# Attention over 64 heads on one core: Exp over three PSUM banks at a time, shared rotating banks, split opening and split last tile

## The chip, the core and the metric

The kernel runs on one core of a Trainium2 chip. The metric is the device time of one execution in microseconds (us); lower is better. A core has five engines that run at the same time and wait for each other through semaphores: TensorE (PE, matrix multiplication; PEld is its weight load), VectorE (DVE), ScalarE (ACT), GpSimd (POOL) and SyncE (SP, which here issues DMAs). Matrix products land in PSUM, a memory of 128 partitions with eight banks of 512 fp32 values each.

## The reference

Softmax attention for 8 batches of 8 heads, 512 queries and 512 keys of 64 values each, in fp32:

```python
def reference(q, k, v):               # each [8, 8, 512, 64]
    scale = 1.0 / np.sqrt(q.shape[-1])
    scores = np.einsum('bhqd,bhkd->bhqk', q, k) * scale
    scores = scores - scores.max(axis=-1, keepdims=True)
    attn = np.exp(scores)
    attn = attn / attn.sum(axis=-1, keepdims=True)
    return np.einsum('bhqk,bhkd->bhqd', attn, v).astype(np.float32)
```

## The kernel before

The 64 heads are worked as 32 pairs. For a pair `g`, one DMA each brings q, k and v of both heads (256 KB each, `load`, L56), five pairs ahead at the start of every pair. POOL casts them to fp16 (`cast`: q and k at L69, v at L73). The v tile has a 65th column of ones, so that the product with it also gives the row sums of the softmax. PE transposes q and k in eight 128x128 pieces into one PSUM bank (`transpose`, L87), and DVE copies the result to the tile `tqk` (L90), where head A lies on partitions 0 to 63 and head B on 64 to 127.

The work then goes by steps `t`: a step is one chunk of 128 keys (`c`, four of them) of one pair. `scores` (L102) makes two matmuls, one for each head, into the two banks of a tile `st`, with keys on the partitions and the 512 queries along the row. `softmax` (L112) is one ACT instruction: exp of both banks, 1024 values per partition, written as fp16 to `pt`. `weigh` (L123) multiplies, for each head and each quarter of the queries, the chunk of `pt` with v: eight matmuls of 65 columns that add into two banks `ps_o`, one for each head, over the four chunks. After the fourth chunk `finish` has DVE take the reciprocal of the sums (L141) and multiply (L142), and SP store the pair (L148).

PSUM is used as follows: `ps_t` one bank, `ps_st` two tiles of two banks, `ps_o` three banks; all eight are taken. No maximum is subtracted; exp is taken of the scaled scores.

The order on each engine is that of the code (`manual_schedule`): in every step exp of `t`, scores of `t + 1`, weigh of `t - 1`, and in the first three chunks of a pair two or three transposes of pair `g + 2`. So PE has a little of each kind of work in each step. An engine takes its instructions strictly in that order, and the tile pools place the waits: `scores(t + 1)` waits until exp of `t - 1` has emptied its two banks.

Of the kernel before, what the change touches and what calls it, by code (L numbers as in the profile page):

```python
# [1 line left out]

# [5 lines left out]

FP32 = mybir.dt.float32
FP16 = mybir.dt.float16  # L10

EXP = mybir.ActivationFunctionType.Exp
AluOp = mybir.AluOpType


@with_exitstack
def kernel(
    ctx: ExitStack,
    tc: tile.TileContext,
    q: bass.AP,  # L20
    k: bass.AP,
    v: bass.AP,
    out: bass.AP,
):
# [10 lines left out]
    NV = 4  # L35

    cpool = ctx.enter_context(tc.tile_pool(name="att_const", bufs=1))
    lpool = ctx.enter_context(tc.tile_pool(name="att_load", bufs=6))
    xpool = ctx.enter_context(tc.tile_pool(name="att_x", bufs=3))
    ppool = ctx.enter_context(tc.tile_pool(name="att_p", bufs=6))  # L40
    opool = ctx.enter_context(tc.tile_pool(name="att_out", bufs=3))
    pspool = ctx.enter_context(tc.tile_pool(name="att_psum", bufs=1, space=bass.MemoryType.PSUM))

    def src(x, g):
        b, h = g // ppb, 2 * (g % ppb)
        return x[b, h : h + 2].rearrange("h (p i) d -> p h (i d)", i=NI)

    raw = {}

    def load(g):  # L50
        if g >= n_pairs:
            return
        t = []
        for nm, x in (("q", q), ("k", k), ("v", v)):
            r = lpool.tile([P, 2, NI * D], FP32, tag=f"{nm}32", name=f"{nm}32_{g}")
            nc.sync.dma_start(out=r, in_=src(x, g))  # L56
            t.append(r)
        raw[g] = t

    vps = [cpool.tile([P, 2, NI, W], FP16, name=f"vp{n}") for n in range(NV)]  # L60
    halves = {}

    def cast(g):
        if g >= n_pairs:
            return
        q32, k32, v32 = raw.pop(g)
        qk = xpool.tile([P, 2, NI, P], FP16, tag="qk", name=f"qk_{g}")
        for n, r in enumerate((q32, k32)):
            nc.gpsimd.tensor_copy(  # L69
                out=qk[:, n].rearrange("p i (h d) -> p i h d", d=D),  # L70
                in_=r.rearrange("p h (i d) -> p i h d", d=D),
            )
        nc.gpsimd.tensor_copy(  # L73
            out=vps[g % NV][:, :, :, 0:D],
            in_=v32.rearrange("p h (i d) -> p h i d", d=D),
        )
        halves[g] = qk

    tps, tqk = {}, {}

    def transpose(g, lo, hi):
        if g >= n_pairs:
            return
        if lo == 0:
            tps[g] = pspool.tile([P, 2, NI, P], FP16, tag="ps_t", bufs=1, name=f"tps_{g}")
        for n in range(lo, hi):
            nc.tensor.transpose(tps[g][:, n // NI, n % NI, :], halves[g][:, n // NI, n % NI, :], ident)  # L87
        if hi == 2 * NI:
            tqk[g] = xpool.tile([P, 2, S], FP16, tag="tqk", name=f"tqk_{g}")
            nc.vector.tensor_copy(out=tqk[g], in_=tps[g])  # L90

    st, pt, ops = {}, {}, {}
    n_steps = n_pairs * NI

    def scores(t):
        if t >= n_steps:
            return
        g, c = divmod(t, NI)
        st[t] = pspool.tile([P, 2, S], FP32, tag="ps_st", bufs=2, name=f"st_{t}")
        for h in range(2):  # L100
            po = D * h
            nc.tensor.matmul(  # L102
                st[t][:, h, :],
                tqk[g][po : po + D, 1, c * P : (c + 1) * P],
                tqk[g][po : po + D, 0, :],
                start=True,
                stop=True,
            )

    def softmax(t):  # L110
        pt[t] = ppool.tile([P, 2, S], FP16, tag="pt", name=f"pt_{t}")
        nc.scalar.activation(out=pt[t], in_=st.pop(t), func=EXP, scale=scale)  # L112

    def weigh(t):
        g, c = divmod(t, NI)
        if c == 0:
            ops[g] = [
                pspool.tile([P, NI, W], FP32, tag="ps_o", bufs=3, name=f"o_{g}_{h}")
                for h in range(2)
            ]  # L120
        for h in range(2):
            for i in range(NI):
                nc.tensor.matmul(  # L123
                    ops[g][h][:, i, :],
                    pt[t][:, h, i * P : (i + 1) * P],
                    vps[g % NV][:, h, c, :],
                    start=(c == 0 and i == 0),
                    stop=(c == NI - 1),
                    skip_group_check=True,
                )  # L130
        del pt[t]
        if c == NI - 1:
            finish(g)

    def finish(g):
        b, hA = g // ppb, 2 * (g % ppb)
        o_sb = opool.tile([P, 2, NI, D], FP32, tag="o_sb", name=f"osb_{g}")
        rcp = opool.tile([P, 2, NI], FP32, tag="rcp", name=f"rcp_{g}")
        for h in range(2):
            o = ops[g][h]  # L140
            nc.vector.reciprocal(out=rcp[:, h, :], in_=o[:, :, D : D + 1])  # L141
            nc.vector.tensor_tensor(  # L142
                out=o_sb[:, h],
                in0=o[:, :, 0:D],
                in1=rcp[:, h, :].broadcast_to([P, NI, D]),
                op=AluOp.mult,
            )
        nc.sync.dma_start(  # L148
            out=out[b, hA : hA + 2].rearrange("h (p i) d -> p h (i d)", i=NI),
            in_=o_sb,  # L150
        )
        del ops[g]

    AHEAD = 5
    with tc.manual_schedule():
        load(0)
        load(1)
        ident = cpool.tile([P, P], FP16, name="ident")
        make_identity(nc, ident)
        for n in range(NV):  # L160
            nc.vector.memset(vps[n][:, :, :, D:W], 1.0)  # L161
        warm = cpool.tile([P, 1], FP32, name="warm")
        nc.vector.memset(warm, 0.0)
        nc.scalar.activation(out=warm, in_=warm, func=EXP, scale=scale)  # L164
        for g in range(2, AHEAD):
            load(g)
        cast(0)
        cast(1)
        transpose(0, 0, 2 * NI)
        scores(0)  # L170
        transpose(1, 0, 2 * NI)
        for t in range(n_steps):
            g, c = divmod(t, NI)
            if c == 0:
                cast(g + 2)
                load(g + AHEAD)
            softmax(t)
            scores(t + 1)
            if t > 0:
                weigh(t - 1)  # L180
            if c < NI - 1:
                transpose(g + 2, 3 * c, min(3 * c + 3, 2 * NI))
        weigh(n_steps - 1)


# [1 line left out]
_INS = ['q', 'k', 'v']  # L187
_OUTS = [((8, 8, 512, 64), 'float32')]


# [23 lines left out]
```

## Time and profile before

| | |
|---|---|
| median of 3 runs | 133.63 us (133.58 to 134.33) |
| the profiled execution, its own time | 133.69 us |
| span of its instructions | 131.8 us |
| ACT busy | 119.4 us, 91% of the span, 130 instructions |
| PE busy | 112.5 us, 85%, 1536 matmuls |
| DVE busy | 58.1 us, 44% |
| POOL busy | 56.9 us, 43% |
| DMA | 33.82 MB, 257 GB/s on average |

The busy time of an engine is the union of its instructions. An ACT instruction that is handed over while the one ahead still runs counts from its hand-over, so the mean of one exp is longer than the distance from one to the next; the distance is what counts in a row of them. The chain of waits follows the work that ended last back to the start: a line of it says from when on, and how long, which instruction held the end back. Times in views are from the start of the span.

### The profile page before, as it was taken

The page shows a single profiled execution, that of the slowest core. Times are in us where ns is not written, and L with a number is a line of the kernel's source. Part 1 is how long each engine was busy: PE and PEld are TensorE (multiplying, and loading weights), DVE is VectorE, ACT ScalarE, POOL GpSimd, SP SyncE. Part 2 cuts the span into 40 slices and gives each one's busy share as a digit, 9 for nine tenths or more (in the row PEclk, how much of TensorE's full clock was granted, in tenths as well). Part 3 has the DMA queues.
Part 4 walks back from the last instruction along what each step waited for, and adds up shares of the span by engine and source line. Part 5 has one row for each costly group of instructions (what it writes and reads, how often), then busy time and mean ns, then how long its engine had stood idle before and what let it go on. Part 6 is the DMA issues. An engine that isn't in the chain of part 4 may idle for free.

```text
span 131.8 us, 3961 instructions
## 1 busy us (share of the span) xinstructions
PE 112.5 (85%) x1536; PEld 71.2 (54%) x1536; DVE 58.1 (44%) x165; ACT 119.4 (91%) x130; POOL 56.9 (43%) x102
## 2 busy tenths in 40 slices
PE   0479999999999999999999999999999999998840
PEld 0225665656556556565655656556565665655530
DVE  0220545544455445554445544554444554455230
ACT  4056999999999999999999999999999999999960
POOL 2578874444455554444445555444444555100000
PEclk9999999999999999999999999999999999999995
DMA  4999999989889879969988989969999982122222
GB/s 116 298 343 349 348 353 371 360 263 296 288 290 308 280 239 306 318 174 341 355 274 291 310 247 286 310 210 274 359 293 307 292 267 86 55 80 80 85 82 80
DMA packets 34836, 33.82 MB, mean 257 GB/s; under 512 B 2049, under 2 KB 34817, under 8 KB 34817
## 3 DMA queue, kind: packets, MB, share of 16 engines
q1 hardware_dynamic: 34816, 33.56, 79.3%
q8 instruction: 12, 0.20, 0.7%
q14 instruction: 8, 0.06, 0.1%
HBM read 25.17 MB, written 8.39 MB: 255 GB/s over the span
## 4 chain that ended last, share of the span: by engine, by line
ACT 72%; issue 10%; PE 8%; DMA 4%; SPq 2%; DVE 1%; POOL 0%
ACT pt L112 72%; DMA q<-in_q_dram 4%; PE st L102 4%; PE o L123 3%; SPq L56 2%; PE tps L87 1%; DVE osb L142 1%; POOL qk L69 0%; DVE rcp L141 0%
## 5 line engine op out<-in xcount | busy, mean ns | idle before, releaser
L112 ACT ACTIVATE pt<-st 128x1024 f16<-128x1024 f32 x128 | 117.9, 1197 | 7.1 <-PE st L102 7.0
L102 PE MATMUL st<-tqk 64*128 64x512 f16 x256 | 51.1, 387 | 9.0 <-ACT pt L112 6.0
L123 PE MATMUL o<-vp,pt 128*128 128x65 f16 x1024 | 54.2, 196 | 0.8 <-ACT pt L112 0.7
L123 PEld LDWEIGHTS <-pt 128*128 128x128 f16 x1024 | 38.5, 98 | 30.1 <-issue 29.0
L73 POOL CAST vp<-v 128x512 f16<-128x512 f32 x32 | 19.8, 619 | 52.8 <-PE o L123 51.1
L90 DVE COPY tqk<-tps 128x1024 f16<-128x1024 f16 x32 | 22.1, 692 | 36.0 <-PE tps L87 36.0
L87 PE MATMUL tps<-ident,qk 128*128 128x128 f16 x256 | 31.0, 227 | 5.4 <-POOL qk L69 5.2
L102 PEld LDWEIGHTS <-tqk 64*128 64x128 f16 x256 | 22.2, 93 | 19.4 <-issue 6.1
L142 DVE TENSOR_TENSOR osb<-o,rcp 128x256 f32<-128x256 f32 x64 | 27.1, 424 | 2.5 <-DMA out_dram<-osb 0.3
L141 DVE RECIPROCAL rcp<-o 128x4 f32<-128x4 f32 x64 | 11.3, 177 | 31.4 <-PE o L123 31.4
L69 POOL CAST qk<-q 128x512 f16<-128x512 f32 x32 | 19.7, 616 | 3.2 <-DMA q<-in_q_dram 3.0
L87 PEld LDWEIGHTS <-qk 128*128 128x128 f16 x256 | 16.5, 101 | 7.0 <-POOL qk L69 7.0
L69 POOL CAST qk<-k 128x512 f16<-128x512 f32 x32 | 19.7, 617 | 0.5
L164 ACT ACT_TABLE_LOAD x1 | 1.3, 1283 | 0.7 <-PEq L198 0.7
L161 DVE MEMSET vp<- 128x8 f16 x4 | 0.2, 65 | 0.8 <-PEq L198 0.8
masks.py:197 POOL MEMSET ident<- 128x128 f16 x1 | 0.2, 205 | 0.3 <-POOLq L198 0.3
masks.py:199 POOL TENSOR_SCALAR_AFFINE_SELECT ident<-ident 128x128 f16<-128x128 f16 x1 | 0.3, 294 | 0.1
L164 ACT ACTIVATE warm<-warm 128x1 f32<-128x1 f32 x1 | 0.2, 202 | 0.0
L198 POOL MEMSET const-float32-0.0<- 128x1 f32 x1 | 0.1, 100 | 0.2 <-issue 0.2
L198 POOL MEMSET const-bfloat16-1.0<- 128x1 bf16 x1 | 0.1, 103 | 0.0
L198 POOL MEMSET const-uint8-127<- 128x1 uint8 x1 | 0.1, 102 | 0.0
L198 POOL MEMSET const-float32-1.0<- 128x1 f32 x1 | 0.1, 100 | 0.0
(1 smaller groups left out, 0.1 us busy)
## 6 DMA issues: line engine op xcount, KB each, us to landing
q<-in_q_dram SPq DMA_DIRECT2D x32, 256.0 KB, 4.1
k<-in_k_dram SPq DMA_DIRECT2D x32, 256.0 KB, 4.4
v<-in_v_dram SPq DMA_DIRECT2D x32, 256.0 KB, 4.7
out_dram<-osb SPq DMA_DIRECT2D x32, 256.0 KB, 3.3
```

What stands on the lines that cost most here:

```text
L56: nc.sync.dma_start(out=r, in_=src(x, g))
L69: nc.gpsimd.tensor_copy(out=qk[:, n].rearrange("p i (h d) -> p i h d", d=D), in_=r.rearrange("p h (i d) -> p i h d", d=D),)
L73: nc.gpsimd.tensor_copy(out=vps[g % NV][:, :, :, 0:D], in_=v32.rearrange("p h (i d) -> p h i d", d=D),)
L87: nc.tensor.transpose(tps[g][:, n // NI, n % NI, :], halves[g][:, n // NI, n % NI, :], ident)
L90: nc.vector.tensor_copy(out=tqk[g], in_=tps[g])
L102: nc.tensor.matmul(st[t][:, h, :], tqk[g][po : po + D, 1, c * P : (c + 1) * P], tqk[g][po : po + D, 0, :], start=True, stop=True,)
L112: nc.scalar.activation(out=pt[t], in_=st.pop(t), func=EXP, scale=scale)
L123: nc.tensor.matmul(ops[g][h][:, i, :], pt[t][:, h, i * P : (i + 1) * P], vps[g % NV][:, h, c, :], start=(c == 0 and i == 0), stop=(c == NI ...
L141: nc.vector.reciprocal(out=rcp[:, h, :], in_=o[:, :, D : D + 1])
L142: nc.vector.tensor_tensor(out=o_sb[:, h], in0=o[:, :, 0:D], in1=rcp[:, h, :].broadcast_to([P, NI, D]), op=AluOp.mult,)
L164: nc.scalar.activation(out=warm, in_=warm, func=EXP, scale=scale)
L198: nc = _bacc.Bacc("TRN2", target_bir_lowering=False, num_devices=1)
```

## The change

The unit of the softmax is now one head's chunk (512 values, one bank), 256 of them, in the same sequence as before (head A and head B of chunk 0, of chunk 1, and so on). They are taken in groups: one of two units, 84 of three, two of one. `scores`, `softmax` and `pt` go by groups, so a group can hold units of two pairs, and a group's heads are A, B, A or B, A, B. `ps_st` is two tiles of three banks. The two banks that are left, `ps_x`, rotate between all other users: the eight transposes of a pair take one, the output of one head takes the next.

The transposes of a pair are therefore issued in one run of eight, and `attend` issues the sixteen matmuls of a head's output at once, when all its four chunks are through exp. Both are put on a list (`work`) and taken from it under an allowance (`credit`) that grows by 0.42 for each unit and holds at most 2.0.

The opening casts and transposes the first pair in parts on three engines (`open_first`), with k of the first pair loaded through ACT's DMA queue, and sixteen matmuls of the identity stand ahead of it on PE. In the last pair the last chunk is two groups of one unit, and each head has a store of its own. Loads run six pairs ahead, q and k are cast three pairs ahead, and the pools `att_x`, `att_p`, `att_out`, `att_load` and the ring of v tiles are larger by one or two.

```diff
+    G = 3
+    NV = 5
+    AHEAD = 6
...
+    def aux(shape, dt, name):
+        return pspool.tile(shape, dt, tag="ps_x", bufs=2, name=name)
+
+    def transpose(g):
...
+        ps = aux([P, 2, NI, P], FP16, f"tps_{g}")
+        for n in range(2):
+            for i in range(NI):
+                nc.tensor.transpose(ps[:, n, i, :], halves[g][:, n, i, :], ident16)
...
+        nc.vector.tensor_copy(out=tqk[g], in_=ps)
+
+    def open_first(g):
...
+        cast(nc.scalar.copy, 1, 0, 1)
+        cast(nc.vector.tensor_copy, 0, 0, NI)
+        cast(nc.gpsimd.tensor_copy, 1, 1, NI)
+        pk = aux([P, NI, P], FP16, f"tk_{g}")
+        pq = aux([P, NI, P], FP16, f"tq_{g}")
+        nc.tensor.transpose(pk[:, 0, :], qk[:, 1, 0, :], ident16)
+        nc.scalar.copy(out=tqk[g][:, 1, 0:P], in_=pk[:, 0, :])
+        for i in range(NI):
+            nc.tensor.transpose(pq[:, i, :], qk[:, 0, i, :], ident16)
+        nc.vector.tensor_copy(out=tqk[g][:, 0, :], in_=pq)
+        for i in range(1, NI):
+            nc.tensor.transpose(pk[:, i, :], qk[:, 1, i, :], ident16)
+        nc.vector.tensor_copy(out=tqk[g][:, 1, P:S], in_=pk[:, 1:NI, :])
+
+    sizes = [2] + [G] * ((n_units - 4) // G) + [1, 1]
...
-        st[t] = pspool.tile([P, 2, S], FP32, tag="ps_st", bufs=2, name=f"st_{t}")
-        for h in range(2):
+        st[j] = pspool.tile([P, G, S], FP32, tag="ps_st", bufs=2, name=f"st_{j}")
+        for x in range(sizes[j]):
+            g, r = divmod(firsts[j] + x, UPP)
+            c, h = divmod(r, 2)
...
+        nc.scalar.activation(out=pt[j][:, 0:n], in_=st.pop(j)[:, 0:n], func=EXP, scale=scale)
...
+    def attend(g, h):
+        o = aux([P, NI, W], FP32, f"o_{g}_{h}")
+        weigh(g, h, o, range(NI))
+        finish(g, h, o, (0, 2) if h == 1 else None)
...
+        load(0, (nc.sync, nc.scalar, nc.sync))
...
+        warm = pspool.tile([P, G, S], FP32, tag="ps_st", bufs=2, name="warm")
+        for n in range(16):
+            nc.tensor.matmul(warm[:, 0, 0:P], ident16, ident16, start=True, stop=True)
+        open_first(0)
+        scores(0)
+        cast_qk(1)
+        cast_v(0)
+        cast_qk(2)
+        cast_v(1)
+        scores(1)
+        transpose(1)
+
+        work = deque()
+        credit = 0.0
+        for j, n in enumerate(sizes):
+            softmax(j)
+            if j > 0:
+                scores(j + 1)
+            if j > 0:
+                for u in range(firsts[j - 1], firsts[j - 1] + sizes[j - 1]):
+                    g, r = divmod(u, UPP)
+                    if r == 0:
+                        cast_qk(g + 3)
+                        cast_v(g + 2)
+                        load(g + AHEAD)
+                    if r == 2 and g + 2 < n_pairs:
+                        work.append((transpose, g + 2))
+                    if r >= UPP - 2 and g < n_pairs - 1:
+                        work.append((attend, g, r - UPP + 2))
+            credit = min(credit + 0.42 * n, 2.0)
+            while work and credit >= 1.0:
+                f, *a = work.popleft()
+                f(*a)
+                credit -= 1.0
...
+                last = [aux([P, NI, W], FP32, f"o_{g}_{h}") for h in range(2)]
+                for h in range(2):
+                    weigh(g, h, last[h], range(NI - 1))
+        for h in range(2):
+            weigh(g, h, last[h], [NI - 1])
+            finish(g, h, last[h], (h, h + 1))
```

Three places show what this does to the order on the engines. In the rows a name ends in its index (pair, or step or group) and a running number of the buffer.

On ACT at the start of the program before, a table load, a first exp of one element and then one exp for each step (`pt_0` is step 0):

```order
L164 ACT_TABLE_LOAD
L164 ACTIVATE warm_100<-warm_100 128x1
L112 ACTIVATE pt_0_164<-st_0_140 128x1024
L112 ACTIVATE pt_1_173<-st_1_166 128x1024
L112 ACTIVATE pt_2_191<-st_2_175 128x1024
```

The same place on ACT now (`tk_0` is the bank with the transposed k of the first pair):

```order
L63 DMA k32_0_82<-in_k_dram 128x2x256
L200 ACT_TABLE_LOAD
L200 ACTIVATE small_96<-small_96 128x1
L108 CAST qk_0_146<-k32_0_82 128x128
L119 COPY tqk_0_147<-tk_0_151 128x128
L152 ACTIVATE pt_0_190<-st_0_164 128x1024
L152 ACTIVATE pt_1_192<-st_1_175 128x1536
```

ACT has a DMA issue, a cast and a copy ahead of its first exp, and from the second exp on 1536 values in each.

On PE in the middle of a pair before, from the last transpose of a step through the scores of step 8 to the outputs of step 6:

```order
L87 MATMUL tps_3_251<-ident_91,qk_3_221 128x128
L102 LDWEIGHTS tqk_2_206
L102 MATMUL st_8_292<-tqk_2_206 128x512
...
L123 LDWEIGHTS pt_6_273
L123 MATMUL o_1_0_260<-vp1_74,pt_6_273 128x65
...
L123 MATMUL o_1_1_261<-vp1_74,pt_6_273 128x65
```

On PE now, from the end of one head's outputs through group 8, whose first unit is of pair 2 and the others of pair 3, to the transposes of pair 4 behind it:

```order
L160 MATMUL o_1_1_343<-vp1_74,pt_5_300 128x65
L141 LDWEIGHTS tqk_2_223
L141 MATMUL st_8_366<-tqk_2_223 128x512
L141 LDWEIGHTS tqk_3_298
L141 MATMUL st_8_366<-tqk_3_298 128x512
...
L97 LDWEIGHTS qk_4_279
L97 MATMUL tps_4_370<-ident16_86,qk_4_279 128x128
```

Scores come in threes, and behind each three stands either nothing, the eight transposes of a pair, or the outputs of both heads of a pair (32 matmuls) in one stretch.

On PE at the end of the program, now: the scores of the last two groups stand side by side (group 85 is the last chunk of head A, group 86 that of head B), behind them the outputs of the chunks before (24 matmuls, of which the first are shown):

```order
L141 MATMUL st_85_2597<-tqk_31_2485 128x512
L141 LDWEIGHTS tqk_31_2485
L141 MATMUL st_86_2601<-tqk_31_2485 128x512
L160 LDWEIGHTS pt_83_2547
L160 MATMUL o_31_0_2603<-vp1_74,pt_83_2547 128x65
```

Before, the outputs of the earlier chunks were issued step by step, and only the eight matmuls of the last chunk stood behind the last exp; now the last chunk's four of head A and four of head B stand behind those 24.

More of the change, by code (lines that the diff above doesn't have):

```diff
@@ L1 @@
+from collections import deque
 from contextlib import ExitStack
@@ L82, in transpose @@
         if g >= n_pairs:
             return
[L84 to L93, printed above, removed]
@@ L97, in scores @@
+    sizes = [2] + [G] * ((n_units - 4) // G) + [1, 1]
+    assert sum(sizes) == n_units
+    firsts = [sum(sizes[:j]) for j in range(len(sizes))]
+    where = {f + x: (j, x) for j, (f, s) in enumerate(zip(firsts, sizes)) for x in range(s)}
+    st, pt = {}, {}
+    def scores(j):
+        if j >= len(sizes):
             return
[L98 to L100 removed]
+        st[j] = pspool.tile([P, G, S], FP32, tag="ps_st", bufs=2, name=f"st_{j}")
+        for x in range(sizes[j]):
+            g, r = divmod(firsts[j] + x, UPP)
+            c, h = divmod(r, 2)
@@ L154, with finish @@
-    AHEAD = 5
+    def finish(g, h, o, store):
+        if h == 0:
+            o_sb[g] = opool.tile([P, 2, NI, D], FP32, tag="o_sb", name=f"osb_{g}")
+        rcp = opool.tile([P, NI], FP32, tag="rcp", name=f"rcp_{g}_{h}")
+        nc.vector.reciprocal(out=rcp, in_=o[:, :, D:W])
+        nc.vector.tensor_tensor(
+            out=o_sb[g][:, h],
+            in0=o[:, :, 0:D],
+            in1=rcp.broadcast_to([P, NI, D]),
+            op=AluOp.mult,
+        )
+        if store:
+            lo, hi = store
+            nc.sync.dma_start(
+                out=rows(out, g, lo, hi),
+                in_=o_sb[g][:, lo:hi].rearrange("p h i d -> p h (i d)"),
+            )
@@ L163 @@
-        nc.vector.memset(warm, 0.0)
-        nc.scalar.activation(out=warm, in_=warm, func=EXP, scale=scale)
-        for g in range(2, AHEAD):
+        small = cpool.tile([P, 1], FP32, name="small")
+        nc.vector.memset(small, 0.0)
+        nc.scalar.activation(out=small, in_=small, func=EXP, scale=scale)
+        for g in range(1, AHEAD):
             load(g)
-        cast(0)
-        cast(1)
-        transpose(0, 0, 2 * NI)
+        warm = pspool.tile([P, G, S], FP32, tag="ps_st", bufs=2, name="warm")
```

123 lines of the change are left out of this document (47 added, 76 removed).

## The prediction

> **What bounds the kernel now.** I read the page first: its groups by line and its chain of waits.
>
> ```profile
> ACT 72%; issue 10%; PE 8%; DMA 4%; SPq 2%; DVE 1%; POOL 0%
> L112 ACT ACTIVATE pt<-st 128x1024 f16<-128x1024 f32 x128 | 117.9, 1197 | 7.1 <-PE st L102 7.0
> L123 PE MATMUL o<-vp,pt 128*128 128x65 f16 x1024 | 54.2, 196 | 0.8 <-ACT pt L112 0.7
> L90 DVE COPY tqk<-tps 128x1024 f16<-128x1024 f16 x32 | 22.1, 692 | 36.0 <-PE tps L87 36.0
> L142 DVE TENSOR_TENSOR osb<-o,rcp 128x256 f32<-128x256 f32 x64 | 27.1, 424 | 2.5 <-DMA out_dram<-osb 0.3
> ```
>
> The chain is exp on ACT. Its 7.1 us of idle time are one stretch, as the timeline of ACT in the first 15 us shows: start, duration, and in brackets the idle time before it.
>
> ```profile
> 2.03 0.20 ACT L164 ACTIVATE warm<-warm 128x1 f32<-128x1 f32 x1
> 7.09 1.02 ACT L112 ACTIVATE pt<-st 128x1024 f16<-128x1024 f32 x1 [4.86 <-PE st L102]
> 9.15 1.02 ACT L112 ACTIVATE pt<-st 128x1024 f16<-128x1024 f32 x1 [1.04 <-PE st L102]
> 10.87 1.02 ACT L112 ACTIVATE pt<-st 128x1024 f16<-128x1024 f32 x1 [0.70 <-PE st L102]
> 12.28 3.08 ACT L112 ACTIVATE pt<-st 128x1024 f16<-128x1024 f32 x3 [0.39 <-PE st L102]
> ```
>
> From 12.3 us on ACT has no gaps to speak of. The chain (start, duration) in the stretch from 63 to 97 us is exp after exp, and the groups of ACT from 64.6 to 95.6 us count 35 of them:
>
> ```profile
> 63.59 0.87 ACT pt L112
> ...
> 94.76 0.87 ACT pt L112
> L112 ACT ACTIVATE pt<-st 128x1024 f16<-128x1024 f32 x35 | 32.5, 1289 | 0.0
> ```
>
> So 34 distances take 94.76 - 63.59 = 31.17 us: 0.917 us for an exp of 1024 values. 128 of them are 117.3 us. The last one ends at 127.24 us, and 127.24 - 117.3 leaves 9.9 us ahead of an unbroken row. I use the sixth exp, which by the waits between the first ones follows unbroken at 14.34 (12.28 + two more, the last of the three ending 3.08 later at 15.36 and lasting 1.02): 14.34 - 5 x 0.917 = 9.76 us is the start of an unbroken row that would end alike. Behind the last exp stand 131.8 - 127.24 = 4.56 us.
>
> The kernel's time is thus an opening of 9.76, a row of exps of 117.3, and a tail. The change touches all three.
>
> **The row of exps: -2.85 us (0 to -3.9).** 256 units of 512 are made in 84 exps of 1536, one of 1024 and two of 512, 87 instructions for 128. What is saved is the fixed part of 41. The trace has two sizes: one element took 0.20, 1024 alone took 1.02. That gives (1.02 - 0.20) / 1023 = 0.80 ns for an element, and 0.917 - 1024 x 0.0008 leaves 0.10 fixed in a row. An exp of 1536 is then 0.917 + 512 x 0.0008 = 1.327. If nothing were fixed it would be 1.5 x 0.917 = 1.375. I take 1.34, near the lower end, because a one-element instruction that takes 0.2 shows that something is fixed, and a little above it because that instruction read another memory straight behind a table load. Sum: 84 x 1.34 + 0.92 + 2 x 0.50 = 114.5, against 117.3; the ends are 113.4 and 117.3.
>
> [...]
>
> This holds only while the scores of a group are there in time. The timeline of PE in one step (start, duration of the run):
>
> ```profile
> 60.01 0.28 PE L87 MATMUL tps<-ident,qk 128*128 128x128 f16 x2
> 61.27 0.39 PE L102 MATMUL st<-tqk 64*128 64x512 f16 x2 [0.18 <-ACT pt L112]
> 61.59 0.42 PE L123 MATMUL o<-vp,pt 128*128 128x65 f16 x8
> 61.85 0.33 PE L87 MATMUL tps<-ident,qk 128*128 128x128 f16 x3
> 62.18 0.39 PE L102 MATMUL st<-tqk 64*128 64x512 f16 x2
> ```
>
> Two scores are through in 0.39, so the two heads run side by side; they hold PE for 61.59 - 61.27 = 0.32, eight outputs for 0.26, and a transpose more costs 0.33 - 0.28 = 0.05. A group of three holds it for at most 0.64: its third matmul is of the same head as the first, and I count it as another pair. Sixteen outputs are 0.52, eight transposes about 0.55 with the change of operands. In eight groups (three pairs) PE needs 8 x 0.64 + 6 x 0.52 + 3 x 0.55 = 9.9 us, ACT 8 x 1.34 = 10.7. PE fits, with 8% to spare.
>
> The bursts: the scores of a group may start when the exp two ahead has ended, and ACT needs them 1.34 later. They take 0.32 + 0.39 to the end of the last and some 0.1 of signals, so PE may be 0.5 late. A group with both heads' outputs holds PE for 0.64 + 1.04 = 1.68, which makes the next 0.34 late: covered. DVE has per pair 0.69 + 2 x (0.20 + 0.42) = 1.9 of 3.57 us (the 0.20 is a row of the tail, below), POOL's three casts of 0.62 are unchanged, and loads and casts are a pair earlier; these I cost at nothing, hidden behind exp. If exp were not the bound, PE would be next.
>
> **The opening: -2.0 us (-2.75 to -0.75).** The rows it rests on, of SP, POOL and PE:
>
> ```profile
> 0.74 0.43 SPq L56 DMA_DIRECT2D q<-in_q_dram  x1
> 1.23 0.46 SPq L56 DMA_DIRECT2D k<-in_k_dram  x1
> 3.64 0.61 POOL L69 CAST qk<-q 128x512 f16<-128x512 f32 x1 [2.34 <-DMA q<-in_q_dram]
> 4.37 0.62 POOL L69 CAST qk<-k 128x512 f16<-128x512 f32 x1
> 7.28 0.62 POOL L69 CAST qk<-k 128x512 f16<-128x512 f32 x1
> 9.86 0.62 POOL L69 CAST qk<-k 128x512 f16<-128x512 f32 x1
> 4.31 1.34 PE L87 MATMUL tps<-ident,qk 128*128 128x128 f16 x8 [4.31 <-POOL qk L69]
> 6.44 0.61 PE L102 MATMUL st<-tqk 64*128 64x512 f16 x2 [0.79 <-DVE tqk L90]
> 10.76 0.62 PE L123 MATMUL o<-vp,pt 128*128 128x65 f16 x8
> 11.63 0.61 PE L102 MATMUL st<-tqk 64*128 64x512 f16 x2
> 12.94 0.43 PE L102 MATMUL st<-tqk 64*128 64x512 f16 x2
> ```
>
> PE runs at half its pace until about 12.6 us: scores take 0.61 there and 0.39 later, and outputs follow each other every (0.62 - 0.19) / 7 = 0.06 instead of 0.03.
>
> First exp: the cast of k starts 0.73 behind that of q, with POOL idle between them, although k was issued 0.49 behind; so the transfers themselves take the time, and a second queue brings both no sooner than 4.3. From there q decides: its cast on DVE (between 0.42, half as many values, and 0.69, twice as many but shorter ones; I take 0.55), four transposes to 5.6, half a copy of 0.69 to 6.05, scores of 0.61 to 6.7. k's first piece on ACT (0.20 + 127 x 0.0008 = 0.3 each for cast and copy) is done by 5.4. So the first exp starts at 6.7 instead of 7.09. The sixteen warm-up matmuls take at most 16 x 1.34 / 8 = 2.7 us by the row of eight transposes, and PE has nothing else before 4.6; they cost nothing.
>
> Then: scores of group 1 wait for nothing new and end near 7.7; exp 1 ends near 9.1. Next on PE stand the transposes of pair 1, and behind them the scores of group 2. k of pair 1 is cast at 7.90 as now; half the transposes to 8.5, the scores at half pace to 9.7. Here ACT waits 0.6, and the scores queued behind are what is late. Exp 2 starts at 9.75, exp 5 is due at 9.75 + 3 x 1.34 = 13.8. Ahead of its scores stand the first burst of 32 outputs, from 12.2: 0.95 at full pace, 1.9 at half, then scores of 0.75 to 1.15. Exp 5 can start between 14.0 and 15.3, which is 0.2 to 1.5 late; I take 0.25, since the rows show full pace from 12.6 on. The row of exps then starts, unbroken, at 9.75 - 0.92 - 1.34 + 0.25 = 7.75 instead of 9.76. If PE ran at full pace from the first scores on it would be 7.0, with the whole burst at half pace 9.0.
>
> **The tail: -0.2 us (-0.5 to +0.3).** The chain behind the last exp:
>
> ```profile
> 125.94 1.30 ACT pt L112
> 127.29 0.31 PE o L123 x4
> 127.62 0.20 DVE rcp L141
> 128.39 0.42 DVE osb L142
> ```
>
> From its end (127.24) to the end of DVE (128.81) are 1.57 us, and two heads' divisions, 1.19 of them, follow each other. Now the last exp, of 512, ends 1.0 behind that of group 84. PE in that time has the scores of group 86 (0.35) and 24 outputs (0.75) ahead of the last eight (0.25): 1.4 with signals. The two divisions then start at about 1.45 and end at 2.65, that is 1.65 behind the last exp instead of 1.57. What is gained is the last transfer, half as long, some 0.3.
>
> **The sum.** -2.85 - 2.0 - 0.2 = -5.05 us, against the profiled execution's own 133.69 (span 131.8 and 1.89 around it): 128.6. Its time is that of the median to 0.06. All lower ends together give 126.5, all upper ends 133.2.
>
> **Rivals.** *Slower: the burst waits for its bank.* Both heads' outputs and the transposes share two banks, and DVE must empty the one two back: 0.20 + 0.42 and signals, some 0.7. If head B's output had to wait that long, the group with the burst would be 1.68 + 0.7 - 1.34 = 1.04 late, 0.5 more than ACT can bear; 32 x 0.5 = 16 us, 144.6. It decides from 5.05 / 32 = 0.16 a pair on. Against it: the bank two back belongs to transposes issued a group earlier, and PE has 2.3 us from their end until head B. *PE is the bound:* with 0.33 for three transposes as in the row, eight take 0.88, and three pairs need 10.9 instead of 10.7: 116.1 for the row, 130.2; that lies in the range. *Nothing fixed is saved:* 131.4; the 0.20 of one element speaks against it. *The first burst runs at half pace:* 129.9; for it speaks that PE's pace changed only at 12.6. *All lower ends:* 126.5. *PE falls to half pace for good:* PE would need up to twice 9.9 for three pairs, 19.8 x 32 / 3 = 211 for the row, 225 in all. The windows of the profile show the clock granted in full although PE has gaps in every fourth step:
>
> ```profile
> 38.00:96.00 58.00, 54.02 (x763) 34.64 (x759) 28.87 (x80) 58.00 (x65) 27.06 (x48) 1.00 0.90 286
> ```
>
> The third number from the end, 1.00, is that clock, and PE (the first busy time) was busy 54.02 of 58 us. [...]
>
> **Chances.** Forecast (127.5 to 129.5, 128.6 likeliest) 0.58; first burst at half pace, with a stall or two more, to 131: 0.16; nothing fixed saved 0.08; all lower ends 0.05; a bank or PE in the way 0.11, of which 0.05 end near the old time and 0.06 beyond it; clock lost 0.02. A measurement of this kernel tells some 1% from no change. Faster by more than that: 0.58 + 0.16 + 0.08 + 0.05 = 0.87; within it 0.05; slower 0.08. The range from 126.5 to 131.5 leaves out the last two cases, 0.13.
>
> **What would show it.** Right: exps of 1536 follow each other every 1.33 to 1.35 us from the sixth on, PE's scores wait for ACT in every group, the first exp starts between 6.3 and 7.0, and ACT's idle time ahead of exp 2 is about 0.6. Wrong: distances above 1.375, idle time of ACT before exps in the middle released by PE, PE waiting for DVE ahead of outputs, scores of 0.61 behind 14 us, or a tail longer than 4.6 us.

## The result and the profile after

The changed kernel takes 128.35 us in the median of four runs (128.08 to 129.81), the kernel before 133.61 beside it. The ratio is 0.962, with a 95% interval of 0.954 to 0.971. Ratios, here and below, leave out runs that are over 1.5% above the fastest run of their kernel. The profiled execution took 128.08, with a span of 126.3 where the one before had 131.8.

From the page of the changed kernel, its first line, its chain and its two largest groups:

```profile
span 126.3 us, 3890 instructions
ACT 71%; issue 16%; PE 5%; DMA 3%; DVE 2%
L152 ACT ACTIVATE pt<-st 128x1536 f16<-128x1536 f32 (+2 forms) x87 | 115.0, 1619 | 1.5 <-PE st L141 1.5
L141 PE MATMUL st<-tqk 64*128 64x512 f16 x256 | 51.9, 386 | 14.0 <-ACT pt L152 11.8
```

Exp on ACT still carries the chain. What ACT waited for ahead of an exp fell from 7.1 to 1.5 us, and PE now waits 11.8 us for ACT in front of scores (before: 6.0): PE has more room, not less.

The timeline of ACT at the start (start, duration, idle time before it in brackets):

```profile
4.46 0.30 ACT L108 CAST qk<-k 128x128 f16<-128x128 f32 x1 [1.72 <-DMA k<-in_k_dram]
5.14 0.27 ACT L119 COPY tqk<-tk 128x128 f16<-128x128 f16 x1 [0.38 <-PE tk L118]
6.69 2.37 ACT L152 ACTIVATE pt<-st 128x1024 f16<-128x1024 f32 x2 [1.29 <-PE st L141]
9.28 6.82 ACT L152 ACTIVATE pt<-st 128x1536 f16<-128x1536 f32 x5 [0.22 <-PE st L141]
```

The first exp starts at 6.69, the third at 9.28 after a wait of 0.22, and from there on nothing interrupts the row. PE in the middle of the program:

```profile
64.51 0.59 PE L141 MATMUL st<-tqk 64*128 64x512 f16 x3 [0.20 <-ACT pt L152]
65.03 1.16 PE L160 MATMUL o<-vp,pt 128*128 128x65 f16 x32
66.12 0.60 PE L141 MATMUL st<-tqk 64*128 64x512 f16 x3
66.65 0.62 PE L97 MATMUL tps<-ident,qk 128*128 128x128 f16 x8
67.20 0.60 PE L141 MATMUL st<-tqk 64*128 64x512 f16 x3
68.54 0.59 PE L141 MATMUL st<-tqk 64*128 64x512 f16 x3 [0.73 <-ACT pt L152]
```

The scores at 64.51 and at 68.54 both waited for ACT and are three groups apart: 4.03 / 3 = 1.343 us for an exp of 1536. Between them the scores at 66.12 came late, because the burst of 32 outputs stood ahead of them; two groups later PE is early again. So the burst makes PE late and ACT does not feel it. Not every pair has such a burst: by the allowance, 21 of the first 31 pairs have both heads' outputs in one stretch, and in every third pair they stand behind two groups, 16 matmuls each (at 39.53 and 40.85 us, for example). The account of the order ahead of the prediction, and the forecast's 32 bursts, left this out.

The difference is split as in the forecast. The unbroken row of exps starts, worked back over the exps ahead of it, at 9.28 - 0.92 - 1.34 = 7.02 (before 9.76, so -2.74). From there to the end of the last exp are 121.94 - 7.02 = 114.92 (before 117.48, so -2.56). Behind the last exp stand 4.32 (before 4.57, so -0.25). The sum is -5.55, all of the difference between the spans.

### The profile page after: what moved, and what is told of

Read it like the earlier page. It is cut to its first block, busy times and chain, and to the rows that moved or that the text cites. A ratio compares the mean times of both kernels' runs of the same rounds, so it can differ in the third digit from the quotient of the medians.

```text
span 126.3 us, 3890 instructions
## 1 busy us (share of the span) xinstructions
PE 105.5 (84%) x1552; PEld 62.1 (49%) x1552; DVE 59.6 (47%) x168; ACT 117.1 (93%) x91; POOL 57.2 (45%) x101
## 4 chain that ended last, share of the span: by engine, by line
ACT 71%; issue 16%; PE 5%; DMA 3%; DVE 2%
ACT pt L152 71%; DMA k<-in_k_dram 3%; PE st L141 3%; DVE osb L174 1%; PE o L160 1%; PE tps L97 1%; DVE rcp L173 0%; PE tq L121 0%; DVE tqk L122 0%; ACT qk L108 0%; PE tk L118 0%
## 5 line engine op out<-in xcount | busy, mean ns | idle before, releaser
L152 ACT ACTIVATE pt<-st 128x1536 f16<-128x1536 f32 (+2 forms) x87 | 115.0, 1619 | 1.5 <-PE st L141 1.5
L141 PE MATMUL st<-tqk 64*128 64x512 f16 x256 | 51.9, 386 | 14.0 <-ACT pt L152 11.8
L160 PEld LDWEIGHTS <-pt 128*128 128x128 f16 x1024 | 33.7, 98 | 18.5 <-issue 16.0
L160 PE MATMUL o<-vp,pt 128*128 128x65 f16 x1024 | 38.8, 194 | 0.0
L99 DVE COPY tqk<-tps 128x1024 f16<-128x1024 f16 x31 | 21.4, 691 | 17.1 <-PE tps L97 17.1
L141 PEld LDWEIGHTS <-tqk 64*128 64x128 f16 x256 | 11.8, 93 | 24.8 <-issue 15.9
L97 PEld LDWEIGHTS <-qk 128*128 128x128 f16 x248 | 14.2, 99 | 13.5 <-issue 9.7
L97 PE MATMUL tps<-ident,qk 128*128 128x128 f16 x248 | 19.6, 223 | 0.0
L205 PE MATMUL warm<-ident 128*128 128x128 f16 x16 | 1.9, 312 | 1.4 <-POOL ident masks.py:199 1.4
L205 PEld LDWEIGHTS <-ident 128*128 128x128 f16 x16 | 1.6, 146 | 1.4 <-POOL ident masks.py:199 1.4
L118 PEld LDWEIGHTS <-qk 128*128 128x128 f16 x1 | 0.1, 105 | 1.8 <-ACT qk L108 1.8
```

Of the source, the lines that this page charges most:

```text
L97: nc.tensor.transpose(ps[:, n, i, :], halves[g][:, n, i, :], ident16)
L99: nc.vector.tensor_copy(out=tqk[g], in_=ps)
L141: nc.tensor.matmul(st[j][:, x, :], tqk[g][po : po + D, 1, c * P : (c + 1) * P], tqk[g][po : po + D, 0, :], start=True, stop=True,)
L152: nc.scalar.activation(out=pt[j][:, 0:n], in_=st.pop(j)[:, 0:n], func=EXP, scale=scale)
L160: nc.tensor.matmul(o[:, i, :], pt[j][:, x, i * P : (i + 1) * P], vps[g % NV][:, h, c, :], start=(c == 0 and i == 0), stop=(c == NI - 1), s ...
L205: nc.tensor.matmul(warm[:, 0, 0:P], ident16, ident16, start=True, stop=True)
```

## Experiments

### Groups of two instead of three

```diff
-    G = 3
+    G = 2
```

> The changed kernel with groups of two units instead of three: exp over two banks, everything else (shared banks, bursts, opening, last pair) as changed. Theory A, that the row of exps is shorter because there are fewer instructions with a fixed part of 0.06 each: exps of 1024 follow each other every 0.917 again, 126 of them and three others make a row of about 117.4 instead of 114.7, and the time is 2.6 us above the changed kernel, some 131.0. Theory B, that the gain comes from the order of the work and the opening, with the size of an exp of no account: the time stays at 128.4.

It took 138.85 us, ratio 1.034 (1.024 to 1.043): slower than the kernel before, which neither theory had. The stretch from 38 to 96 us (its length, then busy time and instructions of PE, PEld, DVE, ACT and POOL, granted clock, DMA share, GB/s):

```profile
38.00:96.00 58.00, 46.77 (x719) 29.47 (x718) 26.76 (x76) 56.14 (x61) 25.42 (x44) 1.00 0.87 272
```

ACT is busy 56.14 of 58. This is PE in one pair, in the timeline of the same kernel:

```profile
61.00 0.39 PE L141 MATMUL st<-tqk 64*128 64x512 f16 x2 [0.20 <-ACT pt L152]
61.91 0.39 PE L141 MATMUL st<-tqk 64*128 64x512 f16 x2 [0.52 <-ACT pt L152]
62.24 1.16 PE L160 MATMUL o<-vp,pt 128*128 128x65 f16 x32
63.33 0.81 PE L141 MATMUL st<-tqk 64*128 64x512 f16 x4
64.90 0.39 PE L141 MATMUL st<-tqk 64*128 64x512 f16 x2 [0.21 <-ACT pt L152]
```

From 61.00 to 64.90 is one pair, 3.90 us. Scores that waited for ACT follow at 0.91, so exps of 1024 have their old distance of 0.917, four of them 3.67; the other 0.23 are lost once for each pair, behind the burst (the trace shows 0.12 of it as idle time of ACT; the rest is that an exp behind a gap takes 1.02, 0.10 more than the distance in a row). Scores and burst hold PE from 61.91 to 63.33, 1.42 us against an exp of 0.92: half a microsecond late, more than two banks cover. Here all 31 pairs ahead of the last have such a burst: 31 waits of 0.23 are 7.1, and the fixed part of the additional exps is 2.6; together they are nearly all of the 10.2 us between the spans of this kernel and the changed one. Theory A is right on the row and had left out what the size of the exp does for the burst: groups of three save fixed parts, and they leave the room that lets both heads be worked in one go. The loss belongs to bursts on two banks, not to two banks alone: the kernel before spreads its outputs over the steps, and its exps of 1024 follow each other every 0.917.

### The old opening in the changed kernel, and no warm-up

The first edit, shown here, loads the first pair on one queue, casts, transposes and copies it whole, and has no warm-up; the second leaves out only the warm-up.

```diff
-        load(0, (nc.sync, nc.scalar, nc.sync))
+        load(0)
...
-        warm = pspool.tile([P, G, S], FP32, tag="ps_st", bufs=2, name="warm")
-        for n in range(16):
-            nc.tensor.matmul(warm[:, 0, 0:P], ident16, ident16, start=True, stop=True)
-        open_first(0)
+        cast_qk(0)
+        transpose(0)
```

> The changed kernel with the first pair opened as before: all its loads on SyncE, q and k cast whole by POOL, eight transposes and one copy by VectorE, and no warm-up matmuls. Theory A, that the opening is worth what its steps cost: first exp at 7.1 instead of 6.7, PE at half pace until about 12.6, so the first burst of 32 outputs holds up an exp by over 1 us; the unbroken row starts 1.5 to 2.0 later, time about 130.2. Theory B, that the opening before was slow because of the transposes and outputs that stood between the scores there, not because of how the first pair was cast: time within 0.5 of the changed kernel, under 129.

> The changed kernel without the sixteen identity matmuls at the start, nothing else. Theory A, that they are what brings PE to full pace at 9.0 instead of 12.6: scores are still 0.6 each at 10 us, the third exp starts 0.3 to 0.5 later, the first burst holds up an exp by about 1 us, time 1.2 to 1.7 above the changed kernel. Theory B, that the denser work of the new opening does it by itself: scores are 0.39 from 9 us on as with the warm-up, time unchanged within 0.3.

With the old opening it took 129.01 us, ratio 0.963 (0.956 to 0.970). The first exp starts at 6.98, the third at 9.83, so the row starts at 7.57: 0.55 later than in the changed kernel's profile and 2.2 earlier than before the change. That is far from theory A's 1.5 to 2.0, and near theory B, whose bound for the time (under 129) it just misses. What casts and copies in parts are worth by themselves is not shown: in four profiles of kernels with the changed opening and groups of three the third exp starts between 9.28 and 9.61, and in a second profile of the changed kernel at 9.85, later than here; only the first exp, at 6.69 to 6.84 in those five, is earlier in each. Without the warm-up it took 128.30, ratio 0.958 (0.950 to 0.967); scores were at 0.39 from 9.7 us on, the row started at 7.24. This is theory B again: no gain of the sixteen matmuls shows, and no cost.

### The order of the opening alone, in the kernel before

```diff
         scores(0)
+        scores(1)
         transpose(1, 0, 2 * NI)
...
-            scores(t + 1)
+            if t > 0:
+                scores(t + 1)
...
-            if c < NI - 1:
+            if g == 0 and c > 0:
+                transpose(g + 2, 3 * c - 3, min(3 * c, 2 * NI))
+            if g > 0 and c < NI - 1:
                 transpose(g + 2, 3 * c, min(3 * c + 3, 2 * NI))
```

> The kernel before with only the order of its opening changed: scores of step 1 stand directly behind those of step 0, and the transposes of pair 2 come one step later than elsewhere. Casts, copies, exps of 1024 and all else as before. Theory A, that most of the opening's gain comes from what stands between the first scores on PE: the second exp starts at about 8.1 instead of 9.15, and the unbroken row 0.8 to 1.5 earlier than 9.76; ratio 0.990 to 0.994. Theory B, that the split casts and copies are what counts: the row starts within 0.3 of 9.76, ratio 1.00.

It took 132.33 us, ratio 0.987 (0.980 to 0.994), a little more than theory A had. This is ACT at its start:

```profile
6.95 1.94 ACT L112 ACTIVATE pt<-st 128x1024 f16<-128x1024 f32 x2 [4.72 <-PE st L102]
9.26 1.02 ACT L112 ACTIVATE pt<-st 128x1024 f16<-128x1024 f32 x1 [0.37 <-PE st L102]
10.67 1.02 ACT L112 ACTIVATE pt<-st 128x1024 f16<-128x1024 f32 x1 [0.39 <-PE st L102]
11.90 4.81 ACT L112 ACTIVATE pt<-st 128x1024 f16<-128x1024 f32 x5 [0.20 <-PE st L102]
```

The wait of 1.04 ahead of the second exp is gone, those behind it add up to 0.96 (before: 1.20), and the span is 130.4, 1.4 below the 131.8 before. This is theory A: of the 2.74 us of the opening, 1.4 are to be had by order alone, without any new cast, copy or bank. What the larger exps and the parts of the opening share of the rest was not taken apart.

### k of the first pair on SyncE's queue

```diff
-        load(0, (nc.sync, nc.scalar, nc.sync))
+        load(0)
```

> The changed kernel with k of the first pair issued from SyncE again, second behind q, instead of from ScalarE's queue. Theory A, as forecast, that the transfers and not the issue set when q and k are there: the first exp starts within 0.2 of 6.7, and the time stays within 0.4 of 128.4. Theory B, that the second queue brings k earlier: k's cast and the first exp come 0.5 later, time about 128.9.

It took 129.78 us in two runs, ratio 0.967 (0.958 to 0.976). The first exp started at 6.53, so theory B falls; but the time is above what either theory had. The third exp started at 10.5, since q of pair 1 came late. These are the rows of POOL in this kernel, and behind them those in the changed one:

```profile
7.50 0.61 POOL L74 CAST qk<-q 128x512 f16<-128x512 f32 x1 [2.67 <-DMA q<-in_q_dram]
8.23 0.61 POOL L74 CAST qk<-k 128x512 f16<-128x512 f32 x1
```

```profile
5.98 0.61 POOL L74 CAST qk<-q 128x512 f16<-128x512 f32 x1 [0.98 <-DMA q<-in_q_dram]
6.79 0.61 POOL L74 CAST qk<-k 128x512 f16<-128x512 f32 x1 [0.20 <-DMA k<-in_k_dram]
```

In the trace v of pair 0 landed 2.45 us behind k here, and 0.75 behind in the changed kernel. The same kernel was run again, with the changed kernel beside it:

> The kernel with k of the first pair on SyncE's queue once more. Theory A, that with all first loads on one queue the third transfer comes late (v of pair 0 landed 1.2 to 2.5 us behind k in the four profiles of that kind, 0.75 behind with k on ScalarE's queue), and q and k of pair 1 with it: v lands over 1.1 behind k again, and the time is 0.5 to 1.5 above the changed kernel beside it. Theory B, that the 129.8 of the first try came from a late change of PE's pace alone (14.5 us): time within 0.4 of the changed kernel.

> The changed kernel once more, to stand beside the others on the same chip and to see what of its opening repeats. Theory A, that the pace of PE changes at a moment that differs from run to run (8.8 us in its profile, but 11.2 to 15.0 in others with the same opening): the change comes at another time, after 9.5, and exp 2 starts at 9.5 to 9.6. Theory B, that 8.8 belongs to this program: again 8.8, exp 2 at 9.3. Time 128.1 to 129.8 in either.

The kernel with k on SyncE took 128.39 to 130.62 us in four runs, ratio 0.962 (0.957 to 0.966); the changed kernel took 128.30 us, ratio 0.959 (0.955 to 0.963). In the kernel with k on SyncE v landed 2.07 behind k again, and q of pair 2 was there between 8.8 and 9.7 us in the five profiles with all first loads on one queue, between 8.2 and 9.0 in nine with k on ACT's. So the pause in the transfers is mostly longer with one queue; that the time differs by it the ratios do not settle, since their intervals meet. In the changed kernel's own second profile the pause came too, one transfer later (q of pair 1 landed 1.52 behind v of pair 0).

That second profile, of an execution of 129.81, also shows where it lost its 1.7 us against the first. PE at its start:

```profile
8.78 1.88 PE L141 MATMUL st<-tqk 64*128 64x512 f16 x6
11.57 1.03 PE L141 MATMUL st<-tqk 64*128 64x512 f16 x3
12.53 1.89 PE L160 MATMUL o<-vp,pt 128*128 128x65 f16 x32
14.35 0.60 PE L141 MATMUL st<-tqk 64*128 64x512 f16 x3
```

The same place in the first profile:

```profile
10.78 0.59 PE L141 MATMUL st<-tqk 64*128 64x512 f16 x3 [0.38 <-ACT pt L152]
11.30 1.16 PE L160 MATMUL o<-vp,pt 128*128 128x65 f16 x32
```

There three scores take 0.59 and the first burst 1.16. In the second profile PE keeps half its pace until 14.2, the first burst takes 1.89, and the sixth exp starts at 14.99 instead of 13.28. This is theory A: the moment belongs to the execution, not to the program. Each trace has records of the granted clock, and they begin at this moment: at 8.9, 10.9, 11.1, 12.2, 13.9 and 14.2 us in the six profiles with this opening, k on ACT's queue and sixteen warm-up matmuls.

### The last two units in one group

```diff
-    sizes = [2] + [G] * ((n_units - 4) // G) + [1, 1]
+    sizes = [2] + [G] * ((n_units - 4) // G) + [2]
...
-            finish(g, h, last[h], (h, h + 1))
+            finish(g, h, last[h], (0, 2) if h == 1 else None)
```

> The changed kernel with the last two units in one group (exp of 1024) and one store for both heads of the last pair. Theory A, by the forecast's term for the tail: one fixed part less in the row (-0.06), but eight outputs, two divisions and a store of 256 KB behind the last exp as before the change; 0.2 to 0.4 us slower than the changed kernel. Theory B, that splitting the last tile is of no account since PE's 24 outputs and VectorE's two divisions stand behind the last exp either way: the same within 0.1.

It took 129.11 us, ratio 0.963 (0.955 to 0.972); its four runs lie between 128.42 and 130.24, so the time does not decide. Measured in the traces from the end of the last exp of 1536, the program has 5.47 us left here and 5.38 in the changed kernel. This is theory B: the split of the last tile is worth 0.1. Behind the last exp it saves what the forecast said: 4.56 are left here, as before the change (4.57), and 4.32 in the changed kernel. But its two exps of 512 take 1.06 where one of 1024 takes 0.92, and so 0.14 of the 0.24 are paid ahead. The chain at the end of the changed kernel shows what still stands there:

```profile
121.30 0.98 PE o L160 x28
122.28 0.02 issue
122.30 0.19 DVE rcp L173
122.50 0.02 issue
122.52 0.42 DVE osb L174
122.94 0.10 DVE rcp L173
123.04 0.02 issue
123.06 0.42 DVE osb L174
```

PE works through 28 outputs in front of the first division, while the last exp ends at 121.94, and both divisions still follow each other.

### How much more PE can bear

Additional matmuls stand ahead of each head's output and go into the same bank; the real ones overwrite them. There are eight in the first kernel, shown here, and sixteen in the second.

```diff
     def attend(g, h):
         o = aux([P, NI, W], FP32, f"o_{g}_{h}")
+        j, x = where[g * UPP + h]
+        for n in range(8):
+            i = n % NI
+            nc.tensor.matmul(
+                o[:, i, :],
+                pt[j][:, x, i * P : (i + 1) * P],
+                vps[g % NV][:, h, 0, :],
+                start=True,
+                stop=True,
+                skip_group_check=True,
+            )
         weigh(g, h, o, range(NI))
```

> The changed kernel with eight more matmuls of 65 columns in front of each head's output, into the same bank, which the real ones then overwrite: 0.26 us more of PE in every attend, 0.52 in a pair, the burst of 32 becomes 48. Theory A, by what the trace of the changed kernel shows (a group of scores holds PE 0.53, 32 outputs 1.08, eight transposes 0.55: 3.05 of 3.58 us a pair): the burst ends 0.8 late where 0.65 can be borne, so ACT waits once for each pair and a little more, 0.1 to 0.3 a pair, time 132 to 138. Theory B, that PE is as full as the forecast had it (3.3 of 3.57 a pair): PE becomes the bound at 3.8 a pair, 8 us more, 136.5 or above. Theory C, that bursts of any length are covered by the idle time between them: no change.

> The same with sixteen more in each attend, 1.04 us more of PE in a pair. PE is then the bound in any theory, and the distance of the pairs measures what PE needs. Theory A (3.05 us a pair as it is): 4.1 us a pair, 131 for the row instead of 114.9, time about 145. Theory B (3.3 as it is): 4.35 a pair, 139 for the row, about 153.

With eight more it took 134.25 us, ratio 1.000 (0.996 to 1.004); with sixteen more 149.33, in two runs, ratio 1.113 (1.101 to 1.125). The stretch from 38 to 96 us, first of the one with eight, then of the one with sixteen:

```profile
38.00:96.00 58.00, 55.34 (x987) 35.00 (x987) 28.59 (x75) 56.12 (x43) 26.58 (x45) 1.00 0.88 279
```

```profile
38.00:96.00 58.00, 55.44 (x1100) 37.60 (x1097) 25.93 (x68) 50.35 (x37) 23.72 (x40) 1.00 0.74 240
```

With eight, ACT waits 0.16 to 0.22 in two of three pairs, those whose outputs stand in one stretch; with the opening its waits are 5.5 us. This is theory A, and not C. With sixteen, 37 exps in 58 us are 4.18 us for a pair (2.67 exps), of which PE is busy 55.44 / 58, so 4.0: theory A's 4.1 and not 4.35. Less the 1.04 added, the changed kernel needs about 3.0 of PE for a pair where the forecast had 3.3. The time is 4 us above theory A's: 32 pairs at 4.18 instead of 4.1 are 2.6, and one wait of ACT at 15.6 us, behind a first burst that ran at half pace until 13.9, is 1.9. So half a microsecond of PE work more for each pair eats up the whole change: the change stands with 15% of PE's time to spare, and with less than that in the burst.

### A version that is faster than both

Three edits at the ends: v of pairs 0 and 1 is loaded behind q and k of pair 1, there are 32 warm-up matmuls, and some outputs of the last pair go ahead of the last scores.

```diff
...
-        load(0, (nc.sync, nc.scalar, nc.sync))
+        load(0, (nc.sync, nc.scalar, nc.sync), 0, 2)
+        load(1, hi=2)
...
-        for g in range(1, AHEAD):
+        load(0, lo=2)
+        load(1, lo=2)
+        for g in range(2, AHEAD):
...
-        for n in range(16):
+        for n in range(32):
...
-            if j == len(sizes) - 2:
+            if j == len(sizes) - 3:
...
-                for h in range(2):
-                    weigh(g, h, last[h], range(NI - 1))
+                weigh(g, 0, last[0], [0, 1])
+                weigh(g, 1, last[1], [0])
+            if j == len(sizes) - 2:
+                weigh(g, 0, last[0], [2])
+                weigh(g, 1, last[1], [1, 2])
```

> The changed kernel with three edits at its ends: v of pairs 0 and 1 is loaded behind q and k of pair 1; 32 warm-up matmuls instead of 16, so that PE works until the first casts are done; and of the 24 outputs in front of the last eight, the twelve that need only the exp before the last of 1536 go ahead of the scores of the last group. Theory A: k of pair 1 lands near 6.0 instead of 6.7, exp 2 follows exp 1 without the gap of 0.2, and the tail from the last exp of 1536 to the end is 0.3 shorter: 0.5 below the changed kernel, 127.9. If the longer warm-up also brings PE's full pace earlier, the first exp starts at 6.4 and it is 127.6. Theory B: exp 2 is held by half-paced scores and the tail by VectorE's two divisions: within 0.2 of the changed kernel.

It took 127.51 us (127.26 to 129.00), ratio 0.953 (0.949 to 0.957), near theory A's 127.6 with full pace earlier; the changed kernel took 128.30 beside it. Its profile is of the execution of 129.00 and shows two things. First, PE lost its pace again. These are the stretches from 8 to 12 and from 12 to 16 us, with the granted clock third from the end of each line:

```profile
8.00:12.00 4.00, 2.52 (x28) 1.41 (x28) 0.91 (x2) 3.89 (x4) 2.60 (x5) 0.93 1.09 351
12.00:16.00 4.00, 3.86 (x40) 2.19 (x37) 1.91 (x5) 2.65 (x3) 3.05 (x6) 0.65 1.11 350
```

And two rows of PE's timeline there:

```profile
7.42 0.60 PE L141 MATMUL st<-tqk 64*128 64x512 f16 x3
11.35 1.91 PE L160 MATMUL o<-vp,pt 128*128 128x65 f16 x32
```

Scores were at full pace from 5.9 us on. Then PE waited for late data, was busy 2.52 of 4 us, and the granted clock fell to 0.93 and 0.65 in the mean (by its records it was half from 11.43 to 14.84); the burst took 1.91 and ACT waited 1.35. Second, head B's four early outputs waited until 121.9 for VectorE to empty their bank, ahead of the last scores, and the last exp came 0.23 late. The second version leaves those four where they were:

```diff
                 weigh(g, 0, last[0], [0, 1])
-                weigh(g, 1, last[1], [0])
             if j == len(sizes) - 2:
                 weigh(g, 0, last[0], [2])
-                weigh(g, 1, last[1], [1, 2])
+                weigh(g, 1, last[1], range(NI - 1))
```

> As e8_better, but of the twelve outputs moved ahead of the last scores only head A's eight, since head B's four waited there for VectorE to empty their bank (until 121.9) and held up the last exp by 0.23. Theory A, that this wait was all: the last two exps follow each other within 0.03 as in the changed kernel, the time from the end of the last exp of 1536 to the end of the program falls from 5.25 to 5.05, time 127.3. Theory B, that the outputs put behind the scores again cost as much at the end as the wait did: 5.25 again, time within 0.1 of 127.5.

It took 127.13 us (127.02 to 127.56), ratio 0.948 (0.944 to 0.952). The last exps follow each other as in the changed kernel, and from the end of the last exp of 1536 (120.11) to the end (125.25) are 5.14 us: about half of what theory A expected came. Scores were at full pace from 5.8 on and the row started at 8.50 - 0.92 - 1.34 = 6.24, without a gap. Which of the two edits to the opening brought the 0.78 against 7.02 was not taken apart.

## Why the prediction was right

The forecast was 128.6 in a range from 126.5 to 131.5; 128.35 was measured. By its steps:

- *The row of exps, -2.85.* It was -2.56. The distance is 1.343 where 1.34 was taken, and three sizes now fit one line: 512 in 0.49, 1024 in 0.917, 1536 in 1.343, which is 0.426 for 512 values and 0.06 fixed. The lower end of the forecast, 1.327, took too much of the one-element exp for fixed.
- *PE fits beside ACT.* Right, with more room than forecast: a group of three holds PE for 65.03 - 64.51 = 0.52, not 0.64, since the third matmul starts 0.21 behind the first two and the burst 0.31 behind the third, where another pair's 0.32 had been counted for it; per pair PE needs 3.0, not 3.3. The rival of the burst that waits for its bank was not there: PE has no idle time ahead of outputs in the page after (0.0 us for its 1024). What lies near instead is the length of the burst, as the two-bank kernel shows. The forecast had such a burst in each of 32 pairs; there are 21, and the others stand in two halves.
- *The opening, -2.0.* It was -2.74 in the profile and 9.76 - 8.70 = 1.06 less in the second one (14.99 less 0.92 and four times 1.34 is 8.70). The first exp came at 6.69 as forecast (6.7), exp 2 waited less (0.22 instead of 0.6), the first burst cost nothing instead of 0.25. The size was off because the forecast took PE's pace to change at 12.6, from the rows of the trace before (the record there has 13.07); it changed between 8.9 and 14.2 us in the six profiles listed above, at 8.9 in the changed kernel's first. The term held because the forecast's bounds ran over this: 7.0 at full pace, 9.0 with the burst at half pace. That its single value and the median agree so well is partly luck: the row saved 0.29 less than forecast and the opening of this profile 0.74 more. The parts fit in kind: the forecast put 0.4 on casts and copies, by the first exp, and the rest on what stands between the scores; the kernel with the old opening started its row 0.55 later, and order alone brought 1.4.
- *A second queue brings q and k no sooner.* Right: q and k landed at 4.11 and 4.43, against 3.59 and 4.32 before. What was missed is the pause behind the second transfer of one queue: in the trace before, v of pair 0 landed 1.46 behind k.
- *The warm-up costs nothing.* Right; no gain of sixteen shows either (128.30 without them, 128.35 with them).
- *The tail, -0.2.* It was -0.25, and the kernel without the split has it back (4.56). What the forecast left out of this term is that the split also lengthens the row ahead, by 0.14, so only 0.1 is left.
- *Clock lost for good.* It was not; the granted clock was 1.00 from 38 to 96 us. Full pace was lost once for some microseconds, from 11.43 to 14.84 us in the profile of the first improved kernel.

## What to carry to other kernels

Where one engine's row of equal instructions is the bound, fewer and larger ones save their fixed part (0.06 us for an exp here), and the larger window also covers longer bursts on the engine that feeds them: behind a burst of 32 outputs ACT lost 0.23 us with exps of 1024 and nothing with exps of 1536. The second effect can be the larger where the work comes in bursts, as the kernel with two banks shows (7.1 us against 2.6). In an opening, look first at what stands between the first instructions of the bounding engine on the queue that feeds it; reordering costs no bank and no instruction, and brought 1.4 us in the kernel before. Read an opening from more than one execution before its parts are priced: the row of the changed kernel started at 7.02 in one profile and at 8.70 in the other.

## What the runs showed of the hardware

PE starts at half pace in all fourteen profiles; in the kernel before, two scores take 0.61 us there and 0.39 later. The records of the granted clock show when that ends: at 13.07 us in the kernel before, and at 8.9 and 14.2 in two profiles of the changed kernel, one and the same program. In the first of these the record of full clock lasts 116.05 us, to 124.98, behind the last matmul. The one loss, in the first improved kernel, was half clock from 11.43 to 14.84.

How long PE was busy does not tell alone when full clock comes. In the changed kernel's first profile PE was busy 3.08 of the 4 us from 4 to 8, and full clock came at 8.9; in its second PE was busy 3.00 of these and 3.87 of the next four, and full clock came at 14.2. In the first improved kernel PE was busy 2.52 of the 4 us from 8 to 12, and had half clock from 11.43 on; in the second 3.20 of them, with 1.00 granted from 8 to 16. What decides there stays open.

With sixteen warm-up matmuls (1.9 us of PE from 1.36 on) none of the six profiles listed above had full clock before 8.9 us; in the changed kernel without them it came at 9.7. With 32 of them, running until the first casts were done, it came at 4.6 and 4.5 us, ahead of the first scores, in two of two profiles; that it always does is not shown.

The views count the time ahead of a trace's first clock record as full, and so show 1.00 from 4 to 12 us in the kernel before, where two scores take 0.61 instead of 0.39 and the first record is at 13.07: there the durations of the scores tell.

With all first loads on one queue, the transfer behind the first two landed 1.15 to 2.45 us after the second in five profiles, where most of the others follow every 0.75. Why there is a pause, and why it came one or two transfers later in some profiles with two queues, stays open.
